# A hybrid decoder block with 32 experts: the gated down biases added to the residual per tile of tokens, in place of a product in each expert

## The chip, the cores and the metric

The kernel runs on one core of one Trainium2 chip. The metric is the device time of one execution in microseconds (us), from the first to the last instruction of the core with what lies around them; smaller is better. Engines are named as the profile names them: PE (TensorE, matrix products), PEld (its weight loads), DVE (VectorE), ACT (ScalarE), POOL (GpSimd) and SP (SyncE, which here only issues transfers). A trailing q (SPq, POOLq, ACTq) is an engine's own instruction queue, DMA issues included. The 16 DMA engines of the core are shared by all queues.

## The reference, cut to what matters

One decoder block on 512 tokens of width 1024 (a gated linear recurrence and a sliding-window attention, merged and projected by `w_out`), and then a mixture of experts: 32 experts, four of which are chosen for each token. All weights are fp32. Of the block's end:

```python
x = x + g1 * (merged @ w_out[l])
h2 = rms_norm(x, norm2_gain[l]) * (1.0 + sc2) + sh2
x = x + g2 * moe_ffn(h2, ...)

def moe_ffn(h, w_router, b_router, w_up, b_up, w_down, b_down):
    logits = (xf @ w_router + b_router).astype(jnp.float32)
    top_vals, top_idx = lax.top_k(logits, TOP_K)          # TOP_K = 4
    gates = jax.nn.softmax(top_vals, axis=-1)
    ...
    def expert_block(args):
        xb, e = args
        hu = xb @ w_up[e] + b_up[e]                        # 1024 -> 2048
        x_glu = jnp.minimum(hu[:, ::2], SWIGLU_LIMIT)
        x_lin = jnp.clip(hu[:, 1::2], -SWIGLU_LIMIT, SWIGLU_LIMIT)
        act = x_glu * jax.nn.sigmoid(SWIGLU_ALPHA * x_glu) * (x_lin + 1.0)
        return act @ w_down[e] + b_down[e]                 # 1024 -> 1024
    ...
    y = jax.ops.segment_sum(y_buf * w_buf[:, None], tok_buf, num_segments=T + 1)[:T]
```

`w_buf` holds the gates. So each expert's bias `b_down[e]` reaches a token's output multiplied by that token's gate for `e` and by `g2`. The sum of these terms over the experts is a product of the gates (512 x 32, four non-zero in a row) with the biases (32 x 1024), and does not depend on the experts' activations.

## The kernel before, in words

**Weights.** Each expert has eight tiles of `w_up` and four of `w_down`, each 1 MB of fp32 as 128 x 2048. SP issues their transfers in the fixed order up 0 to 7 of expert e, then down 0 to 3 of expert e-1, into a ring of slots: nine of `slot`, `NSB` of `slotb` and `NSC` of `slotc`, 18 together. Some of these slots also hold split tiles. A transfer is issued as soon as the slot that it goes into has been released, and SP's queue is in order, so a late release holds back all transfers behind it.

**Splits.** A tile is split into a high fp16 part (ACT, L341 in the helper `split`) and the low rest (DVE, L346), which also releases the fp32 slot. The fourth down tile of an expert is used in fp32 without a split. `ahead(i)` issues the splits up to six places ahead of the tile that PE is about to use.

**An expert on PE.** `up_k` (L1190) is run eight times, with 48 matmuls each; between them stand the selection products of the next expert's tokens (`pick`, L1150). Then `swiglu` runs on DVE and ACT (L1199 to L1216). The down part of expert e-1 comes after the up part of expert e: `down_bias` (L1225), two matmuls that set the two PSUM banks `pd` to the expert's bias, taken from the 64-row table `bd` (high and low fp16 parts of `b_down`, made in `bias_dn`) by a one-hot column of `E64`; then `down_j` (L1241 in fp16, L1233 in fp32) adds to `pd`; `finish` multiplies with gate and `g2row` into `y` (L1253, DVE) and POOL adds up to 96 rows of `y` into the output in memory with an indirect accumulating transfer (L1245).

**The router stage.** It lies between the block's first half and the experts (380 to 445 us). For each of four tiles of 128 tokens, `logits(t)` multiplies by `w_out` (L903, PE), forms the new residual `x1` (L958 to L961, DVE), transposes it (L968, PE; copies L971 on ACT and L972 on DVE), multiplies by the router weights (L976), and writes `x1` to the output (L983, POOL's queue); `choose(t)` and `gates(t)` find the four experts and their gates on DVE (L987 to L1027). The four tiles of `x` are loaded ahead of the loop, each into its own buffer. In this stage `pre(t)` issues a few splits of the first expert's tiles; a scheduler sets the order on each engine.

**Order.** From `mark` on, just behind the router's loop, PE, DVE and ACT run their instructions in the order in which the program writes them. A wait on one of these engines therefore holds everything behind it. POOL and SP are in order too. At the end stands a loop over experts with more than 96 tokens (overflow), which runs no round in these inputs' profile.

Of the kernel before, what the change touches and what calls it, by code (L numbers as in the profile page):

```python
# [10 lines left out]
F32 = mybir.dt.float32  # L11
F16 = mybir.dt.float16
# [29 lines left out]
def block_body(tc, x, c, positions, w_ada, b_ada, norm1_gain, w_in, lower_bound_logits, hg_norm_gain,  # L42
# [19 lines left out]
    with top:  # L62
# [874 lines left out]
        gs = moe.tile([128, NT, 2], F32, name="gs")  # L937
        ge = moe.tile([128, NT, NE], F32, name="ge")
        GS = 1024.0

        x1s, xas, rss = {}, {}, {}

        for t in range(NT):
            x1s[t] = wk.tile([128, D], F32, name=f"x1_{t}")
            A.dma_start(x1s[t], x2[128 * t:128 * t + 128, :])

        def logits(t, pieces):
# [34 lines left out]
            V.scalar_tensor_tensor(lg[:, t, :], bl[:, :NE], rs[:, 2:3], brow, op0=OP.mult, op1=OP.add)  # L982
            G.dma_start(out2[128 * t:128 * t + 128, :], x1)  # L983

# [33 lines left out]
        def gates(t):  # L1018

            V.tensor_sub(gt[:, t], tv[:, t, 0:4], tv[:, t, 0:1].to_broadcast([128, 4]))  # L1020
            A.activation(gt[:, t], gt[:, t], AF.Exp, accum_out=gs[:, t, 0:1])
            V.reciprocal(gs[:, t, 1:2], gs[:, t, 0:1])
            V.tensor_scalar(gt[:, t], gt[:, t], gs[:, t, 1:2], GS, op0=OP.mult, op1=OP.mult)
            V.tensor_mul(oh[:, t], oh[:, t], gt[:, t, :, None].to_broadcast([128, 4, NE]))
            V.tensor_reduce(ge[:, t, :], oh[:, t].rearrange("p k e -> p e k"), axis=AX.X, op=OP.add)
            V.tensor_copy(aux[:, t, :, 1], ge[:, t, :])
            V.tensor_sub(aux[:, t, :, 2], ge[:, t, :], aux[:, t, :, 1])  # L1027

# [3 lines left out]
        SU = SW * SH2  # L1032
        pmod = moe.tile([64, 1], F32, name="pmod")
        G.iota(pmod[0:32], pattern=[[0, 1]], base=0, channel_multiplier=1, allow_small_or_imprecise_dtypes=True)
        G.iota(pmod[32:64], pattern=[[0, 1]], base=0, channel_multiplier=1, allow_small_or_imprecise_dtypes=True)
        E64 = moe.tile([64, NE], F16, name="E64")
        V.tensor_scalar(E64, iota_e[:64, :], pmod[:, 0:1], 32768.0, op0=OP.is_equal, op1=OP.mult)

        SBD = 1.702 * SW * SACT / 32768.0

# [10 lines left out]
        def bias_dn():  # L1051
            st = ready.pop(("bdn",))
            A.activation(bd, st[:64, :1024], AF.Copy, scale=SBD)
            V.scalar_tensor_tensor(bd[32:64], st[32:64, :1024], SBD, bd[32:64], op0=OP.mult, op1=OP.subtract)
            free(st)
# [32 lines left out]
        def select0(t0, t1):  # L1088
            V.tensor_tensor(sel0[:, t0:t1], iota_c[:, None, :C].to_broadcast([128, t1 - t0, C]),
                            pos[:, t0:t1, 0:1].to_broadcast([128, t1 - t0, C]), op=OP.is_equal)  # L1090

        for t in range(NT):
            if t == NT - 1:
                select0(0, NT - 1)
            logits(t, ((0, D),) if t < NT - 1 else LAST)
            pre(t + 1)
            if t < NT - 1:
                choose(t)
                make_h2(t)
                gates(t)  # L1100
        for j in range(4):
            hl_done(("wo", j))
# [119 lines left out]

        def down_bias(one):
            for u in range(2):
                T.matmul(pd[u][:C, :], lhsT=one.to_broadcast([64, C]), rhs=bd[:, 512 * u:512 * u + 512],  # L1225
                         start=True, stop=False)

        def down_j(w, j, act, act32):
            if j == 3:
                for u in range(2):  # L1230
                    for k in (6, 7):
                        o = 1024 * (k % 2) + 512 * u
                        T.matmul(pd[u][:C, :], lhsT=act32[:, k - 4, :], rhs=w[:, o:o + 512],  # L1233
                                 start=False, stop=(k == KT - 1))
                return
            for k in (2 * j, 2 * j + 1):
                o = 1024 * (k % 2)
                for n, (pa_, pw) in enumerate(PASSES):
                    for u in range(2):
                        c0 = 2048 * pw + o + 512 * u  # L1240
                        T.matmul(pd[u][:C, :], lhsT=act[:, pa_, k, :], rhs=w[:, c0:c0 + 512],  # L1241
                                 start=False, stop=False)

# [103 lines left out]
        for e in range(NEX + 1):  # L1347
            if e < NEX:
                prep = nexts.pop(e + 1, iter(()))
                xg = state[e][0]  # L1350
                for k in range(8):
                    ahead(i)
                    if e > 0 and k in PICK_AT:
                        next(prep, None)
                    up_k(hlmap[("up", e, k)], k, xg)
                    hl_done(("up", e, k))
                    if k == 3 and e in TABLE_AT:
                        next(table)
# [20 lines left out]
            if e > 0:  # L1379
                _, gate, idx = state.pop(e - 1)  # L1380
                down_bias(E64[:, e - 1:e])
                for j in range(4):
# [28 lines left out]
        with tc.For_i(0, nreg, 1) as it:  # L1411
# [39 lines left out]
            swiglu(act, act32)  # L1451
            e1h = moe.tile([64, 1], F16, name="ovh")
            V.tensor_scalar(e1h, pmod, col[:64, 0:1], 32768.0, op0=OP.is_equal, op1=OP.mult)
            down_bias(e1h)
            for j in range(4):
# [18 lines left out]
_OUTS = [((1, 512, 1024), 'float32')]  # L1474
NSB, NSC = 5, 4
LOOK = 6
# [29 lines left out]
```

## Time and profile before

| what | value |
|---|---|
| median of 2 runs | 1498.71 us (1497.76 to 1499.66) |
| profiled execution: its own time | 1499.43 us |
| profiled execution: its span | 1497.6 us |
| mean granted clock of TensorE | 0.981 |
| PE / PEld / DVE / ACT / POOL busy, share of the span | 94% / 69% / 87% / 70% / 22% |
| bytes by the hardware queue of the loads (q1) | 458.78 MB, 78.0% of the 16 engines' span |
| mean DMA rate over the span | 318 GB/s |

The execution has three parts: the block's first half (up to about 380 us), the router stage (to about 445 us), and 32 experts (to the end). Shares over the whole span mix them; the views below are therefore cut to stretches. PEclk is the granted clock as a share of 2.4 GHz. A busy PE in the profile is not a PE at its peak, because ends of matmuls are modelled.

### The profile page before, as it was taken

How to read it: one execution, taken by the hardware profiler on the slowest of the kernel's cores; microseconds unless marked ns; L12 is line 12 of the kernel's file. 1: busy time of each engine (PE TensorE's matmuls, PEld its weight loads, DVE VectorE, ACT ScalarE, POOL GpSimd, SP SyncE). 2: the span in 40 equal slices, each digit the busy share in tenths (PEclk: the TensorE clock that was granted, in tenths of full speed). 3: DMA queues.
4: the chain of work that ended last, by engine and by line, in shares of the span. 5: the costliest groups of instructions: out<-in, count | busy, mean ns of one | idle time of the engine just before them, and what ended most of it. 6: DMA issues, size and time to landing. Idle time of an engine off the chain costs nothing. (4 is left out here: it accounts for less than half of the span.)

```text
span 1497.6 us, 41130 instructions
## 1 busy us (share of the span) xinstructions
PE 1405.6 (94%) x18200; PEld 1039.4 (69%) x18200; DVE 1300.0 (87%) x1457; ACT 1054.6 (70%) x1024; POOL 328.4 (22%) x82
## 2 busy tenths in 40 slices
PE   3979999999978999999989999999999999999994
PEld 2536567444558877788777788877788877788871
DVE  6876677777888999999999999999999999999882
ACT  4556334632448888887978888888888888888860
POOL 1020000010110333322322334212044433215300
PEclk9999999999988999999999999999999999999997
DMA  9822321476758999999999999999999999999971
GB/s 315 276 87 85 113 56 57 138 258 231 292 215 308 390 392 411 406 405 398 393 397 367 405 408 411 401 405 400 406 409 401 408 389 403 397 401 409 391 276 16
DMA packets 113520, 476.44 MB, mean 318 GB/s; under 512 B 10717, under 2 KB 35386, under 8 KB 80538
## 3 DMA queue, kind: packets, MB, share of 16 engines
q1 hardware_dynamic: 106160, 458.78, 78.0%
q0 software_dynamic: 5440, 12.72, 3.9%
q8 instruction: 144, 2.36, 0.6%
q10 hardware_dynamic: 1738, 2.27, 0.5%
q14 instruction: 38, 0.31, 0.1%
HBM read 463.22 MB, written 14.70 MB: 319 GB/s over the span
## 5 line engine op out<-in xcount | busy, mean ns | idle before, releaser
L1190 PE MATMUL pu<-xg,slot 128*128 128x96 f16 x10224 | 465.6, 207 | 8.8 <-issue 7.5
L1190 PEld LDWEIGHTS <-slot 128*128 128x128 f16 x10224 | 449.2, 98 | 25.5 <-issue 21.8
L1245 POOL DMA_INDIRECT out_dram<-y,idx x32 | 295.0, 9219 | 754.4 <-DVE y L1253 740.3
L346 DVE SCALAR_TENSOR_TENSOR slot<-slot,slot 128x2048 f16<-128x2048 f32 (+1 forms) x120 | 271.4, 2271 | 30.9 <-ACT slot L341 30.5
L341 ACT ACTIVATE slot<-slot 128x2048 f16<-128x2048 f32 (+1 forms) x120 | 242.0, 2032 | 68.9 <-DVE slot L346 24.1
L346 DVE SCALAR_TENSOR_TENSOR slot<-slotb,slot 128x2048 f16<-128x2048 f32 x101 | 228.0, 2285 | 8.0 <-ACT slot L341 7.7
L346 DVE SCALAR_TENSOR_TENSOR slot<-slotc,slot 128x2048 f16<-128x2048 f32 x97 | 219.6, 2284 | 11.8 <-ACT slot L341 10.5
L341 ACT ACTIVATE slot<-slotc 128x2048 f16<-128x2048 f32 x97 | 201.6, 2105 | 33.7 <-issue 11.5
L341 ACT ACTIVATE slot<-slotb 128x2048 f16<-128x2048 f32 x101 | 197.1, 1956 | 34.5 <-PE pu L1190 14.6
L1241 PEld LDWEIGHTS <-act 128*96 128x96 f16 x1152 | 140.2, 124 | 116.8 <-issue 17.0
L1241 PE MATMUL pd<-slot,act 128*96 128x512 f16 x924 | 206.4, 380 | 0.0
L701 PE MATMUL mm<-hT,slot 128*128 128x512 f16 x672 | 151.4, 380 | 0.0
L701 PEld LDWEIGHTS <-slot 128*128 128x128 f16 x672 | 65.5, 98 | 77.6 <-issue 2.9
L1150 PE MATMUL gb<-sel,h 128*128 128x96 f16 x1984 | 106.9, 208 | 12.8 <-ACT xg L1157 11.1
L1150 PEld LDWEIGHTS <-h 128*128 128x128 f16 x1984 | 93.1, 99 | 12.7 <-issue 12.5
L1190 PE MATMUL pu<-xg,slotb 128*128 128x96 f16 x2064 | 96.0, 207 | 1.8 <-issue 1.8
L1190 PEld LDWEIGHTS <-slotb 128*128 128x128 f16 x2064 | 91.2, 98 | 5.2 <-issue 4.6
L1233 PE MATMUL pd<-slot,act 128*96 128x512 f32 x144 | 64.7, 592 | 0.0
L785 POOL DMA_DIRECT2D mdram<-mr x8 | 4.7, 592 | 269.5 <-DVE mr L779 206.3
L1157 ACT ACTIVATE xg<-gb 128x384 f16<-128x384 f32 x124 | 59.2, 478 | 1.1 <-PE gb L1150 1.1
L1183 ACT ACTIVATE pu<-bu 128x384 f32<-128x384 f32 x128 | 57.2, 480 | 1.0 <-DVE sg_g L1199 1.0
L1253 DVE SCALAR_TENSOR_TENSOR y<-pd,gate,g2row 96x512 f32<-96x512 f32 x64 | 44.9, 739 | 14.0 <-PE pd L1233 14.0
(339 smaller groups left out, 1637.1 us busy)
## 6 DMA issues: line engine op xcount, KB each, us to landing
slotc<-in_w_up_dram SPq DMA_DIRECT2D x116, 1024.0 KB, 15.4
slot<-in_w_up_dram SPq DMA_DIRECT2D x110, 1024.0 KB, 13.9
slotb<-in_w_down_dram SPq DMA_DIRECT2D x98, 1024.0 KB, 17.6
slotb<-in_w_up_dram SPq DMA_DIRECT2D x30, 1024.0 KB, 12.3
slot<-in_w_down_dram SPq DMA_DIRECT2D x20, 1024.0 KB, 22.4
slot<-in_w_in_dram SPq DMA_DIRECT2D x16, 1024.0 KB, 5.3
slot<-in_w_ada_dram SPq DMA_DIRECT2D x16, 1024.0 KB, 5.5
slotc<-in_w_down_dram SPq DMA_DIRECT2D x10, 1024.0 KB
```

The lines of the kernel that those rows point to most:

```text
L341: A.activation(hi, src, AF.Copy, scale=SW)
L346: V.scalar_tensor_tensor(lo, src, SW, hi, op0=OP.mult, op1=OP.subtract)
L701: T.matmul(bk, lhsT=hl[:, o:o + 128], rhs=hT[:, ph, k, :], start=(k == 0 and n == 0), stop=(k == KT - 1 and n == 2))
L785: G.dma_start(mdram[q:q + 1, 512 * u:512 * u + 512], m)
L1150: T.matmul(bk[:, C * k:C * k + C], lhsT=h2[:, part, t, 128 * kk:128 * kk + 128], rhs=sel[:, t, :], start=(k == 0 and t == 0), stop=(t == N ...
L1157: A.activation(xg[:, part, 4 * u:4 * u + 4, :].rearrange("p k c -> p (k c)"), bk[:, :4 * C], AF.Copy)
L1183: A.activation(pu[i][:, :4 * C].rearrange("p (m c) -> p m c", m=4), b[:, 4 * i:4 * i + 4, None].to_broadcast([128, 4, C]), AF.Copy)
L1190: T.matmul(o, lhsT=hl[:, 2048 * pw + 128 * f:2048 * pw + 128 * f + 128], rhs=xg[:, pa_, k, :], start=False, stop=(k == KT - 1 and n == 2), ...
L1233: T.matmul(pd[u][:C, :], lhsT=act32[:, k - 4, :], rhs=w[:, o:o + 512], start=False, stop=(k == KT - 1))
L1241: T.matmul(pd[u][:C, :], lhsT=act[:, pa_, k, :], rhs=w[:, c0:c0 + 512], start=False, stop=False)
L1245: G.indirect_dma_start(out=out2, out_offset=bass.IndirectOffsetOnAxis(ap=idx[:n, :1], axis=0), in_=y[:n, :], in_offset=None, bounds_check= ...
L1253: V.scalar_tensor_tensor(y[:C, sl], pd[u][:C, :], gate[:C], g2row[:C, sl], op0=OP.mult, op1=OP.mult)
```

## The change: gated biases per tile of tokens

The two matmuls of `down_bias` go out of every expert, with `E64` and `pmod`; the first matmul of `down_j` now starts the bank. In their place:

- `bias_dn` first multiplies the bias table by `g2row` (L1075, DVE), so `bd` holds `g2 * b_down`.
- For tiles 0, 1 and 2 of the tokens, `residual(t)` runs behind `gates(t)`: PE transposes the gates (L1033), ACT and DVE make a high and a low part (L1034, L1035), four matmuls of 512 columns multiply them with `bd` (L1041, L1042), DVE adds the two banks to `x1` (L1053), and only then is `x1` written to the output (L1054).
- Tile 3's `x1` is written without the biases, as before. Its bias products are made while expert 1 runs, into the banks `pd`, and added to the output by one more indirect accumulating transfer, of 128 rows.
- `x1` has two buffers for the four tiles. The load of tile t+1 is issued at the start of round t, from ACT's queue; that of tile 2 waits until tile 0 has been written out, that of tile 3 until tile 1 has.
- `slotb` has six slots instead of five and `slotc` three instead of four; the slots of `slotb` exist in the router stage already.
- Expert 0 issues no splits in its last four rounds, and in expert 31 `ahead` stops earlier, so that some splits stand behind the `swiglu` of these experts.

```diff
@@ router stage
-        for t in range(NT):
-            x1s[t] = wk.tile([128, D], F32, name=f"x1_{t}")
+        def load_x1(t):
+            x1s[t] = wk.tile([128, D], F32, name="x1", bufs=2)
             A.dma_start(x1s[t], x2[128 * t:128 * t + 128, :])
...
-            G.dma_start(out2[128 * t:128 * t + 128, :], x1)
+            if t == NT - 1:
+                G.dma_start(out2[128 * t:128 * t + 128, :], x1)
...
+            V.tensor_copy(ge[:, t, 1, :], ge[:, t, 0, :])
+
+        def gates_T(t, bk, gT):
+
+            T.transpose(bk[:64, :128], ge[:, t].rearrange("p u e -> p (u e)"), ident)
+            A.activation(gT[:, 0], bk[:64, :128], AF.Copy)
+            V.tensor_sub(gT[:32, 1], bk[:32, :128], gT[:32, 0])
+
+        def bias_products(gT, bks):
+
+            for u in range(2):
+                sl = slice(512 * u, 512 * u + 512)
+                T.matmul(bks[u], lhsT=gT[:, 0], rhs=bd[:, sl], start=True, stop=False)
+                T.matmul(bks[u], lhsT=gT[:32, 1], rhs=bd[:32, sl], start=False, stop=True)
+
+        def residual(t):
+
+            gT = wk.tile([64, 2, 128], F16, name="gT")
+            gates_T(t, sd_bank(), gT)
+            bks = [sd_bank(), sd_bank()]
+            bias_products(gT, bks)
+            x1 = x1s[t]
+            for u in range(2):
+                sl = slice(512 * u, 512 * u + 512)
+                V.scalar_tensor_tensor(x1[:, sl], bks[u], 1.0 / (GS * SBD), x1[:, sl], op0=OP.mult, op1=OP.add)
+            G.dma_start(out2[128 * t:128 * t + 128, :], x1)
...
         def bias_dn():
             st = ready.pop(("bdn",))
+            V.tensor_mul(st[:64, :1024], st[:64, :1024], g2row[:64])
             A.activation(bd, st[:64, :1024], AF.Copy, scale=SBD)
             V.scalar_tensor_tensor(bd[32:64], st[32:64, :1024], SBD, bd[32:64], op0=OP.mult, op1=OP.subtract)
...
+        load_x1(0)
         for t in range(NT):
             if t == NT - 1:
                 select0(0, NT - 1)
+            if t < NT - 1:
+                load_x1(t + 1)
             logits(t, ((0, D),) if t < NT - 1 else LAST)
             pre(t + 1)
             if t < NT - 1:
                 choose(t)
                 make_h2(t)
                 gates(t)
+                residual(t)
@@ experts
-        def down_bias(one):
-            for u in range(2):
-                T.matmul(pd[u][:C, :], lhsT=one.to_broadcast([64, C]), rhs=bd[:, 512 * u:512 * u + 512],
-                         start=True, stop=False)
...
                         T.matmul(pd[u][:C, :], lhsT=act[:, pa_, k, :], rhs=w[:, c0:c0 + 512],
-                                 start=False, stop=False)
+                                 start=(k == 0 and n == 0), stop=False)
...
                 for k in range(8):
-                    ahead(i)
+                    if e == NEX - 1:
+                        ahead(min(i, len(order) - 5 - LOOK))
+                    elif e > 0 or k < 4:
+                        ahead(i)
...
+                    if e == 1 and k == 1:
+                        gT = moe.tile([128, 4 * C], F32, name="sg_l").bitcast(F16)[:64, :256]
+                        gT = gT.rearrange("p (q n) -> p q n", q=2)
+                        gates_T(NT - 1, pd[0], gT)
+                    if e == 1 and k == 3:
+                        bias_products(gT, pd)
+                        y = moe.tile([128, D], F32, name="y")
+                        for u in range(2):
+                            V.tensor_scalar(y[:, 512 * u:512 * u + 512], pd[u], 1.0 / (GS * SBD), None, op0=OP.mult)
+                        rix = moe.tile([128, 1], I32, name="idx", bufs=4)
+                        G.iota(rix, pattern=[[0, 1]], base=128 * (NT - 1), channel_multiplier=1)
+                        add_out(y, rix, 128)
...
-                down_bias(E64[:, e - 1:e])
...
-NSB, NSC = 5, 4
+NSB, NSC = 6, 3
```

The first place is DVE in the router stage, behind the gates of tile 0 (`ge`, `aux`); `rs` are the small steps of tile 1's norm, `xat` the low part of its transposed tile. Of the kernel before:

```order
L1025 TENSOR_REDUCE ge<-oh 128x32
L259 TENSOR_SCALAR rs<-rs 128x1
L1026 CAST aux<-ge 128x32
L260 TENSOR_SCALAR rs<-rs 128x1
L1027 TENSOR_TENSOR aux<-ge,aux 128x32
L972 TENSOR_TENSOR xat<-sd,xat 128x512
L261 TENSOR_SCALAR rs<-rs 128x1
L262 TENSOR_SCALAR rs<-rs 128x1
L265 TENSOR_SCALAR rs<-rs 128x1
```

And of the change:

```order
L1027 CAST aux<-ge 128x32
L1029 COPY ge<-ge 128x32
L260 TENSOR_SCALAR rs<-rs 128x1
L1028 TENSOR_TENSOR aux<-ge,aux 128x32
L261 TENSOR_SCALAR rs<-rs 128x1
L262 TENSOR_SCALAR rs<-rs 128x1
L265 TENSOR_SCALAR rs<-rs 128x1
L269 SCALAR_TENSOR_TENSOR rs<-rs 128x1
L1035 TENSOR_TENSOR gT<-sd,gT 32x128
...
L1053 SCALAR_TENSOR_TENSOR x_2893<-sd,x_2893 128x512 x2
L972 TENSOR_TENSOR xat<-sd,xat 128x512
```

A copy of the gates (L1029), the low part of the transposed gates (L1035, which needs PE and ACT first) and two additions to tile 0's `x1` (L1053, which need the bias products) now stand among tile 1's steps, and the copy of `xat` behind them.

The second place is ACT's queue in the router stage, in the change, with the waits: `x_3044` and `x_3194` are the `x1` of tiles 2 and 3, `DMASW2` and `DMASW3` the landing of POOL's writes of tiles 0 and 1.

```order
L1005 ACTIVATE h_2220<-xa 128x1024 [waits DVE_49]
L945 DMA x_3044<-in_x_dram 128x1024 [waits DMAHW0_49,DMASW2_49]
L1022 ACTIVATE gt,gs<-gt 128x4 [waits DVE_49]
L1034 ACTIVATE gT<-sd 64x128 [waits PE_49,Activation_49]
L963 ACTIVATE sqt,rs<-x_3044 128x1024 [waits DMAHW0_49,DVE_49]
L971 ACTIVATE xat<-sd 128x512 [waits PE_49,Activation_49] x2
L945 DMA x_3194<-in_x_dram 128x1024 [waits DMAHW3_49,DMASW3_49,DVE_49]
```

The loads of tiles 2 and 3 stand ahead of the exponential of a later tile's gates (L1022), and the copies of `gT` and `xat` behind it; before, all four loads stood ahead of the first tile's work.

The third place is DVE at the end of expert 31: L1199 and L1226 open its `swiglu`, L1253 and L1275 are the results of experts 30 and 31. Of the kernel before:

```order
L346 SCALAR_TENSOR_TENSOR slotb_2806<-slot_63,slotb_2806 128x2048
L346 SCALAR_TENSOR_TENSOR slotb_2807<-slot_70,slotb_2807 128x2048
L1199 TENSOR_SCALAR sg_g<-pu_3465 128x384
L1199 TENSOR_SCALAR sg_g<-pu_3466 128x384
...
L1216 SCALAR_TENSOR_TENSOR act<-act_21740,act 128x192
L346 SCALAR_TENSOR_TENSOR slot_71<-slotc_3544,slot_71 128x2048
L1253 SCALAR_TENSOR_TENSOR y<-pd_3469,gate,g2row 96x512
L1253 SCALAR_TENSOR_TENSOR y<-pd_3470,gate,g2row 96x512
```

And of the change:

```order
L346 SCALAR_TENSOR_TENSOR slotc_3586<-slotb_2809,slotc_3586 128x2048
L1226 TENSOR_SCALAR sg_g<-pu_3505 128x384
L1226 TENSOR_SCALAR sg_g<-pu_3506 128x384
...
L1243 SCALAR_TENSOR_TENSOR act<-act_21731,act 128x192
L346 SCALAR_TENSOR_TENSOR slot_68<-slot_69,slot_68 128x2048
L346 SCALAR_TENSOR_TENSOR slotb_2807<-slot_64,slotb_2807 128x2048
L346 SCALAR_TENSOR_TENSOR slot_67<-slot_63,slot_67 128x2048
L1275 SCALAR_TENSOR_TENSOR y<-pd_3509,gate,g2row 96x512
```

The splits of the first two down tiles of expert 31 have moved from ahead of its `swiglu` to behind it. Expert 0's `swiglu` moves the other way round the splits too: between the selection matrix for expert 1 (L1172, now L1199) and this `swiglu` stand nine splits in the kernel before and four in the change.

## Rows read from the trace of the kernel before

**Rows 1.** Windows; columns: stretch, length, busy time per engine, granted clock, DMA share, rate.

```profile
400.00:410.00 10.00, 8.00 (x44) 3.98 (x43) 9.96 (x21) 5.08 (x7) 3.84 (x2) 1.00 0.04 16
492.00:554.00 62.00, 62.00 (x996) 50.06 (x994) 60.26 (x51) 53.84 (x47) 22.55 (x2) 1.00 1.00 398
833.00:864.00 31.00, 31.00 (x500) 25.03 (x498) 30.07 (x26) 26.97 (x24) 12.03 (x1) 1.00 1.02 405
1468.00:1475.00 7.00, 6.54 (x15) 2.82 (x15) 0.98 (x2) 0.00 (x0) 1.43 (x1) 0.50 0.23 33
```

**Rows 2.** DMA view, 1000 to 1130 us: queue, packets, MB, share; issues with us to landing.

```profile
q1 hardware_dynamic: 9079, 51.21, 96.5%
q0 software_dynamic: 448, 1.14, 4.4%
...
slotb<-in_w_down_dram SPq DMA_DIRECT2D x13, 1024.0 KB, 20.2
```

**Rows 3.** DMA view, 480 to 483 us: one load on idle queues, with us to landing.

```profile
slotc<-in_w_up_dram SPq DMA_DIRECT2D x1, 1024.0 KB, 4.8
```

**Rows 4.** Timeline of PE, one down part: start, length, line, operation, count.

```profile
787.36 0.63 PE L1225 MATMUL pd<-bd,E 64*96 64x512 f16 x2
787.92 5.38 PE L1241 MATMUL pd<-slot,act 128*96 128x512 f16 x24
```

**Rows 5.** Timeline of DVE, router stage; in brackets: idle before and its releaser.

```profile
387.91 1.29 DVE L958 SCALAR_TENSOR_TENSOR xa<-mm,rrow 128x512 f32<-128x512 f32 x2 [5.00 <-PE mm L903]
...
394.85 0.69 DVE L972 TENSOR_TENSOR xat<-sd,xat 128x512 f16<-128x512 f32 x1 [0.38 <-ACT xat L971]
...
399.76 1.28 DVE L1003 SCALAR_TENSOR_TENSOR xa<-xa,rs,rrow 128x1024 f32<-128x1024 f32 x1
...
410.51 0.20 DVE L1026 CAST aux<-ge 128x32 f16<-128x32 f32 x1
...
417.80 0.68 DVE L960 TENSOR_TENSOR x<-x,xa 128x512 f32<-128x512 f32 x1
...
424.23 0.69 DVE L958 SCALAR_TENSOR_TENSOR xa<-mm,rrow 128x512 f32<-128x512 f32 x1 [1.61 <-PE mm L903]
```

**Rows 6.** DMA view, 374 to 440 us, issues: KB each, median us to landing.

```profile
x<-in_x_dram ACTq DMA_DIRECT2D x4, 512.0 KB, 6.8
...
g2row<-mdram POOLq DMA_DIRECT2D x1, 512.0 KB, 9.6
```

**Rows 7.** DMA view, 404 to 415 us: a write of `x1` on idle queues.

```profile
out_dram<-x POOLq DMA_DIRECT2D x1, 512.0 KB, 3.4
```

**Rows 8.** DMA view, 386 to 396 us: the same write beside weight loads.

```profile
out_dram<-x POOLq DMA_DIRECT2D x1, 512.0 KB, 9.6
```

**Rows 9.** Timeline of POOL: issue of the load of `g2row`.

```profile
380.19 0.55 POOL L885 DMA_DIRECT2D g2row<-mdram  x1 [4.29 <-DMA mdram<-mr]
```

**Rows 10.** Timeline of DVE around the `swiglu` of expert 0.

```profile
472.28 1.01 DVE L1199 TENSOR_SCALAR sg_g<-pu 128x384 f32<-128x384 f32 x2
...
478.90 4.50 DVE L346 SCALAR_TENSOR_TENSOR slot<-slotc,slot 128x2048 f16<-128x2048 f32 x2 [0.96 <-ACT slot L341]
```

**Rows 11.** Timeline of DVE at the end.

```profile
1458.06 2.29 DVE L346 SCALAR_TENSOR_TENSOR slotb<-slot,slotb 128x2048 f16<-128x2048 f32 x1 [1.03 <-ACT slotb L341]
1460.27 1.02 DVE L1199 TENSOR_SCALAR sg_g<-pu 128x384 f32<-128x384 f32 x2
...
1465.38 2.29 DVE L346 SCALAR_TENSOR_TENSOR slot<-slotc,slot 128x2048 f16<-128x2048 f32 x1 [1.28 <-ACTq L1411]
1467.59 1.40 DVE L1253 SCALAR_TENSOR_TENSOR y<-pd,gate,g2row 96x512 f32<-96x512 f32 x2
```

**Rows 12.** Timeline of PE at the end.

```profile
1458.64 3.60 PE L1233 MATMUL pd<-slot,act 128*96 128x512 f32 x8
1468.38 1.24 PE L1225 MATMUL pd<-bd,E 64*96 64x512 f16 x2 [6.14 <-DVE y L1253]
1469.55 8.14 PE L1241 MATMUL pd<-slotb,act 128*96 128x512 f16 x24
```

More of the change, by code (lines that the diff above doesn't have):

```diff
@@ L937, in block_body @@
         gs = moe.tile([128, NT, 2], F32, name="gs")
-        ge = moe.tile([128, NT, NE], F32, name="ge")
+        ge = moe.tile([128, NT, 2, NE], F32, name="ge")
         GS = 1024.0
         x1s, xas, rss = {}, {}, {}
-        for t in range(NT):
-            x1s[t] = wk.tile([128, D], F32, name=f"x1_{t}")
+        def load_x1(t):
+            x1s[t] = wk.tile([128, D], F32, name="x1", bufs=2)
             A.dma_start(x1s[t], x2[128 * t:128 * t + 128, :])
@@ L1024, in gates @@
             V.tensor_mul(oh[:, t], oh[:, t], gt[:, t, :, None].to_broadcast([128, 4, NE]))
-            V.tensor_reduce(ge[:, t, :], oh[:, t].rearrange("p k e -> p e k"), axis=AX.X, op=OP.add)
-            V.tensor_copy(aux[:, t, :, 1], ge[:, t, :])
-            V.tensor_sub(aux[:, t, :, 2], ge[:, t, :], aux[:, t, :, 1])
+            V.tensor_reduce(ge[:, t, 0, :], oh[:, t].rearrange("p k e -> p e k"), axis=AX.X, op=OP.add)
+            V.tensor_copy(aux[:, t, :, 1], ge[:, t, 0, :])
+            V.tensor_sub(aux[:, t, :, 2], ge[:, t, 0, :], aux[:, t, :, 1])
+            V.tensor_copy(ge[:, t, 1, :], ge[:, t, 0, :])
[18 more added lines that the diff above has]
+            G.dma_start(out2[128 * t:128 * t + 128, :], x1)
         bu = moe.tile([128, NE, 16], F32, name="bu")
@@ L1032, in block_body @@
         SU = SW * SH2
[L1033 to L1039, printed above, removed]
+        SBD = 16.0
         def bias_up():
@@ L1451, in block_body @@
             swiglu(act, act32)
-            e1h = moe.tile([64, 1], F16, name="ovh")
-            V.tensor_scalar(e1h, pmod, col[:64, 0:1], 32768.0, op0=OP.is_equal, op1=OP.mult)
-            down_bias(e1h)
             for j in range(4):
```

## Prediction

> **What bounds the kernel now.** I first cut the execution into windows and read busy times beside the DMA share. The reader is to see that no single engine answers for the whole. From 400 to 410 us DVE is busy 9.96 of 10 us and the 16 DMA engines 0.04; in the expert part they change places with a share of 1.00 to 1.02, while PE is busy for 62.00 of 62 and for 31.00 of 31 us as well [rows 1]. So in the expert part two resources look full, and the change takes work from one of them. Next came the DMA view of a stretch in the middle: the weight loads move 51.21 MB in 130 us, and a load lands 20.2 us after its issue [rows 2], against 4.8 us on idle queues [rows 3]. So several earlier loads always wait in the queues: (20.2 - 4.8) us at 2.66 us a load (below) are about six. An expert has twelve loads of 1.049 MB, 12.58 MB; at 51.21/130 = 0.394 MB per us they take 31.9 us, 2.66 each. PE needs 31.00 us for 500 matmuls and an expert has 498, so 30.9 us; DVE is busy 30.07 of the same 31 [rows 1]. DMA is the slowest, by 1.0 us per expert; PE can run full only by eating up the lead of loaded slots. The end is set by when the DMA engines start to run without gaps, the number of bytes from there, and what follows the last load. The router stage, where DVE is full and DMA stands, sets the first; the timelines of DVE and PE at the end show the third.
>
> **The change, part by part.** The sum is made against the profiled execution's 1499.43 us, 0.7 us above the median of 1498.71 of the runs shown.
>
> *Bias products out of the experts.* L1225 starts at 787.36 and the next line at 787.92: 0.56 us [rows 4]. In 32 experts that is 17.9 us less on PE, and PE's need falls from 30.9 to 30.3 us. I cost this at nothing, since the loads' 31.9 us cover it; without that cover it would be the whole 17.9 us.
>
> *Bias table times `g2row`.* `g2row` is issued at 380.19 [rows 9] and lands 9.6 us later [rows 6], at 389.8. Before, DVE's next work began at 387.91, behind 5.00 us of idle time, in which the making of `bd` lay hidden [rows 5]. Now L1075 must wait for `g2row` on DVE, with tile 0's first additions behind it: 1.9 us, or nothing if `g2row` lands sooner because two of the four `x` loads no longer run beside it. I take the middle, 1.0. L1075 and L1077 cover 1024 columns as the 1.28 us row does [rows 5], 1.2 us each by their pitch. Sum 3.4 us, ends 2.4 and 4.3.
>
> *Per tile, three times, on DVE.* Two additions of 512 columns, as the pair at 387.91, 1.29 us; a copy of 32 columns and the low part of the gates, 0.20 us each by the row of the 32-column copy [rows 5]: 1.7 us, 5.1 in all. Then two waits per tile for PE and ACT (transpose and copy; products). The nearest row is the 0.38 us for an ACT copy [rows 5]: six of these are 2.3 us, but small steps of the next tile stand in between, so 1.5; ends 0 and 3. PE and ACT have idle time there and cost nothing more. Of the existing gaps DVE can fill part, such as 1.61 us at 424.23 [rows 5]: minus 1.0, ends 0 and minus 3.1, which grants as much again for gaps that have no row here. Sum 5.6 us.
>
> *Two buffers for `x1`.* The load of tile 2 waits for tile 0's write, and ACT, in order, waits with it: the exponential of tile 1's gates stands behind. The chain is the issue 0.55 [rows 9], a write of 3.4 us on idle queues [rows 7], and a load for which I take the same 3.4: 7.4 us. From the gates of tile 0 at 410.51 to the first addition of tile 2 at 417.80 DVE worked 7.3 us [rows 5]; with the half of tile 1's work that now comes behind L1053 I count about 8. So nothing, with 1 us as upper end; the case of busy queues is a rival. The Trainium skill, page "DMA: Bandwidth & Descriptors", section "Anatomy of one DMA", prices a transfer at 2.0 us plus its bytes at 436 KB per us, which for 512 KB makes 3.2 us. By it no tile would stall; the trace agrees on idle queues with 3.4 us, and not beside weight loads.
>
> *One slot more in the router stage.* One load earlier is worth 1.049/0.394 = 2.7 us if the DMA engines never run dry after it. They do: at about 481 us a load meets empty queues [rows 3]. So nothing; lower end minus 2.7.
>
> *Splits around the `swiglu` of expert 0.* It opened at 472.28, and splits went on at 478.90, 6.6 us later [rows 10]. With five splits of 2.2 us moved behind, it could open at 461.3, and the five end at 461.3 + 6.6 + 11.0 = 478.9: no change, unless PE has not yet finished the last up tile and DVE idles. I take plus 1.0, ends 0 and 2.5.
>
> *The added accumulating transfer.* Four of them take 4.4% of 130 us and 1.14 MB [rows 2], 1.43 us and 0.285 MB each. The new one has 128 rows of 4 KB, 0.52 MB: 2.6 us of full DMA engines, ends 1.4 and 2.8.
>
> *The end.* Before, `swiglu` of expert 31 waited until 1460.27 behind a split that waited for its load; a third split followed at 1465.38, and `y` of expert 30 came at 1467.59, for which PE waited 6.14 us [rows 11, 12]. With `swiglu` ahead of the splits, the third can follow the second at once: it began 7.3 us after it [rows 11] and needs only 2.2, less what ACT's high parts take behind `swiglu`, about 1.2. That makes 3.9 us; PE's expert 30 ends at 1462.2 [rows 12] and forbids more than 5.3. L1225 with its 1.24 us at this place goes too: minus 5.1 in all. If PE's shorter pause leaves its clock at 2.4 GHz, the 24 matmuls that took 8.14 us at a granted 0.50 [rows 1, 12] take 5.38 [rows 4]: up to 2.8 us more. I don't count that. Ends minus 3 and minus 8.
>
> Sum: 3.4 + 5.6 + 0 + 1.0 + 2.6 - 5.1 = +7.5 us; 1499.4 + 7.5 = **1507 us**, 0.55% above the median. With all ends on one side: 2.4 + 2.0 + 0 - 2.7 + 1.4 - 8 = -4.9, so 1494.5; and 4.3 + 8.1 + 1 + 2.5 + 2.8 - 3 = +15.7, so 1515.
>
> **The rivals.** *PE sets the pace.* If loads could run faster whenever PE asks for them faster, all 17.9 us come back: 1507 - 17.9 = 1489 us. For it speaks PE's busy time; against it the 20.2 us from issue to landing, since queues with six loads in them already run as fast as they can. By the Trainium skill, page "Perfetto Trace Analysis", section "Identifying the Most-Contended Engine", the occupancy of 16 DMA engines misleads and the rate is to be read; page "DMA: Bandwidth & Descriptors", section "Measured", has 425 GB/s for a large transfer, so the 405 here would leave 5%. The landing times of this trace speak against that room. Chance 0.09.
>
> *The router stage hides it.* If the scheduler puts the new steps wholly into DVE's gaps and `g2row` lands early, the router costs 2 us in place of 9.0: 1500 us. Against it: DVE's 9.96 of 10 us. Chance 0.17.
>
> *The write of `x1` stalls its next load (slower).* Beside weight loads a write takes 9.6 [rows 8] and a load 6.8 us [rows 6]: 0.55 + 9.6 + 6.8 = 17 us against 8 of cover, 9 us for tile 2 and again for tile 3: 1507 + 18 = 1525 us. It decides as soon as write and load together exceed about 7.5 us. For it: the tenth early load lengthens the traffic into this stage, and ACT is held too. Against it: the DMA share of 0.04 from 400 us on. Chance 0.12.
>
> That the products stay in the experts is excluded by the program: no line multiplies `bd` in the experts but tile 3's.
>
> **How the numbers follow.** Forecast 0.62, rivals 0.09, 0.17 and 0.12. The likeliest case has 1494 to 1515 us. The range reaches to 1490 on the side of the PE rival and to 1520 on that of the stalled loads, and leaves out about half of the first, most of the second and the ends of the likeliest, 0.2 together. A difference of 2% (30 us) is about what a measurement of this kernel tells from no change. Faster by that needs 1469 us, which no case reaches: 0.02. Slower by it needs 1529, which only the stalled loads with further delay reach: 0.04. Within 2%: 0.94.
>
> **What would show it.** Right: the first gapless loads come some 10 us later than before, twelve loads still take 31.9 us, PE shows gaps in the experts, and PE's pause before the last down part shrinks to some 2 us. Wrong: loads per expert faster than 31.9 us; idle time of DVE ahead of L960 for tiles 2 and 3; a router stage as long as before; or DMA engines that run dry for longer after expert 0's `swiglu`.

## The result and the profile after

The changed kernel takes 1522.31 us (median of 2 runs, 1521.99 to 1522.63) against 1498.71: ratio 1.0149, interval 1.0133 to 1.0165 (the two medians alone give 1.0157). The forecast was 1507, its range ended at 1520: slower than forecast by 15 us, and 2 us outside the range.

To see where the time went, I cut each profiled execution at four marks that every version has: the issue of the first of the 384 weight loads of the experts (SP), DVE's step that makes the router's values `lg` of tile 3, the issue of the 38th weight load (in expert 2 to 3, when the loads run without gaps), and that of the 382nd (the third down tile of expert 31). Each entry is a difference of two starts in one trace, in us.

| kernel | to first load | first load to `lg(3)` | `lg(3)` to 38th load | 38th to 382nd load | 382nd load to end | span |
|---|---|---|---|---|---|---|
| before | 364.6 | 75.5 | 71.2 | 922.3 | 64.0 | 1497.6 |
| after | 365.5 | 95.4 | 78.5 | 923.4 | 57.9 | 1520.7 |
| after less before | +0.9 | +19.9 | +7.3 | +1.0 | -6.0 | +23.1 |

The first column, which the change does not touch, tells how far two executions differ anyhow: 364.3 to 366.9 over all versions. The last but two points to what paces the experts: 344 loads take 922.3 us before and 923.4 after, 2.68 us each, though PE is busy for 15 us less in that stretch (890.32 us in place of 905.50). So the loss sits in the router stage and in experts 0 and 1, and a gain at the end.

**The router stage.** Timeline of DVE of the changed kernel, start, length, line, operation, in brackets the idle time before and what ended it. `L1075` is the bias table times `g2row`, `L960` the addition to `x1`; the row at 428.97 is tile 2, that at 449.45 tile 3.

```profile
385.34 1.22 DVE L1075 TENSOR_TENSOR slot<-slot,g2row 64x1024 f32<-64x1024 f32 x1
390.50 0.69 DVE L958 SCALAR_TENSOR_TENSOR xa<-mm,rrow 128x512 f32<-128x512 f32 x1 [3.94 <-PE mm L903]
...
428.97 0.68 DVE L960 TENSOR_TENSOR x<-x,xa 128x512 f32<-128x512 f32 x1
...
438.76 0.25 DVE L982 SCALAR_TENSOR_TENSOR lg<-sd,rs,brow 128x32 f32<-128x32 f32 x1
...
449.45 0.69 DVE L960 TENSOR_TENSOR x<-x,xa 128x512 f32<-128x512 f32 x1 [8.99 <-DMA x<-in_x_dram]
...
460.92 0.25 DVE L982 SCALAR_TENSOR_TENSOR lg<-sd,rs,brow 128x32 f32<-128x32 f32 x1
```

`g2row` makes nobody wait here: `L1075` starts without idle time (in x1_four it waits 0.43 us), and what DVE waits for next is PE, as before the change [rows 5]. Tile 2's addition has no bracket. Tile 3's has 8.99 us, and the releaser is its own load. The queues show why; here POOL, ACT and SP of the changed kernel:

```profile
433.26 0.58 POOL L1054 DMA_DIRECT2D out_dram<-x  x1 [8.74 <-DVE x L1053]
```

```profile
434.37 0.60 ACT L971 ACTIVATE xat<-sd 128x512 f16<-128x512 f32 x1 [1.13 <-PE sd L968]
441.52 0.33 ACTq L945 DMA_DIRECT2D x<-in_x_dram  x1
441.96 2.01 ACT L341 ACTIVATE slot<-slotb 128x2048 f16<-128x2048 f32 x1 [6.99 <-DMA out_dram<-x]
```

```profile
433.34 2.70 SPq L158 DMA_DIRECT2D slot<-in_w_up_dram  x3
436.64 27.68 SPq L158 DMA_DIRECT2D slotc<-in_w_up_dram  x3
```

Tile 1's `x1` is written from 433.26 on. ACT stands behind this write until 441.52, and only then issues tile 3's load, which lands 7.9 us later. Both transfers, 8.2 and 7.9 us, are more than twice as long as a write on idle queues (3.4 us, [rows 7]), and SP starts weight loads again at 433.34: PE has done with the first `w_out` tiles (SP's wait of 44.7 us ended with `L903`), and their slots come free. The windows (columns as in [rows 1]) show the same as a change of traffic in the middle of the stage:

```profile
410.00:430.00 20.00, 15.66 (x99) 7.63 (x97) 17.37 (x51) 4.62 (x11) 4.04 (x3) 0.91 0.15 53
430.00:440.00 10.00, 6.60 (x71) 4.53 (x70) 9.21 (x30) 2.50 (x5) 0.58 (x1) 0.95 0.53 184
440.00:450.00 10.00, 0.18 (x1) 0.00 (x0) 0.98 (x3) 3.15 (x4) 2.11 (x1) 0.50 1.01 426
490.00:552.00 62.00, 53.30 (x911) 45.72 (x912) 57.21 (x41) 51.74 (x41) 14.33 (x2) 0.89 0.85 318
862.00:893.00 31.00, 30.92 (x509) 25.34 (x506) 30.46 (x26) 27.45 (x24) 14.57 (x2) 1.00 1.02 408
```

From 440 to 450 us DVE is busy 0.98 of 10 us and PE 0.18, and TensorE's granted clock is 0.50, its lower level of 1.2 GHz. The DMA share is 1.01: not the queues, but the work stands.

**Experts 0 and 1.** After the change `lg(3)` comes 20.8 us later (460.92 in place of 440.12), so the same work is to be compared 20.8 us later too. Of the kernel before, 62 us from 29 us behind `lg(3)` on:

```profile
469.00:531.00 62.00, 60.55 (x1008) 52.26 (x1008) 58.61 (x56) 52.82 (x51) 12.15 (x1) 0.92 0.93 356
```

Against the row of 490 to 552 us above, the DMA share falls from 0.93 to 0.85: by estimate 0.08 x 62 = 5 us more in which the loads could have run. In the DMA view, 40 slices of 1.5 us each show the holes, first of the kernel before from 469 to 529 us, then of the changed kernel from 490 to 550:

```profile
DMA  9999992047999899999999968999999999999999
```

```profile
DMA  9700496685036999999999999999899999999999
```

DVE of the changed kernel opens expert 0's `swiglu` at 481.39, and then waits:

```profile
481.39 1.02 DVE L1226 TENSOR_SCALAR sg_g<-pu 128x384 f32<-128x384 f32 x2 [1.89 <-PE pu L1217]
...
486.67 0.15 DVE L1192 TENSOR_SCALAR idx<-gb 96x1 int32<-96x1 f32 x1 [3.26 <-ACT xg L1184]
...
491.28 2.29 DVE L346 SCALAR_TENSOR_TENSOR slot<-slotb,slot 128x2048 f16<-128x2048 f32 x1 [0.94 <-ACT slot L341]
```

```profile
483.53 0.49 ACT L1184 ACTIVATE xg<-gb 128x384 f16<-128x384 f32 x1 [5.86 <-PE gb L1177]
```

```profile
491.31 0.26 PE L1217 MATMUL pu<-xg,slot 128*128 128x96 f16 x1 [5.57 <-ACT slot L341]
```

Three engines wait one for another: DVE for ACT's copies of expert 1's selected tokens (`xg`), ACT for PE's selection products, and PE then for the splits, which begin again at 491.28, 9.9 us after `swiglu` opened (6.6 before, [rows 10]). The loads show what that costs: counted from `lg(3)`, the 23rd is issued after 21.9 us and the 24th only after 34.9 (before: 27.9 and 30.1).

**The end.** DVE and PE of the changed kernel:

```profile
1480.90 1.01 DVE L1226 TENSOR_SCALAR sg_g<-pu 128x384 f32<-128x384 f32 x2
...
1486.01 2.29 DVE L346 SCALAR_TENSOR_TENSOR slot<-slot,slot 128x2048 f16<-128x2048 f32 x1 [1.28 <-ACT slot L341]
1488.21 2.28 DVE L346 SCALAR_TENSOR_TENSOR slotb<-slot,slotb 128x2048 f16<-128x2048 f32 x1
1490.42 2.28 DVE L346 SCALAR_TENSOR_TENSOR slot<-slot,slot 128x2048 f16<-128x2048 f32 x1
1492.62 1.40 DVE L1275 SCALAR_TENSOR_TENSOR y<-pd,gate,g2row 96x512 f32<-96x512 f32 x2
```

```profile
1493.51 4.56 PE L1263 MATMUL pd<-slot,act 128*96 128x512 f16 x12 [5.69 <-DVE y L1275]
```

Against [rows 11] the splits follow `swiglu` without a wait for a load, and the time from the 382nd load to the end falls from 64.0 to 57.9 us.

### The profile page after: what moved, and what is told of

The parts are those of the page before. It is cut to its first block, busy times and chain, and to the rows that moved or that the text cites. A ratio compares the mean times of both kernels' runs of the same rounds, so it can differ in the third digit from the quotient of the medians.

```text
span 1520.7 us, 41073 instructions
## 1 busy us (share of the span) xinstructions
PE 1393.5 (92%) x18156; PEld 1034.6 (68%) x18156; DVE 1304.7 (86%) x1473; ACT 1052.9 (69%) x1028; POOL 397.7 (26%) x82
## 3 DMA queue, kind: packets, MB, share of 16 engines
q1 hardware_dynamic: 106160, 458.78, 76.7%
## 5 line engine op out<-in xcount | busy, mean ns | idle before, releaser
L1267 POOL DMA_INDIRECT out_dram<-y,idx x33 | 365.5, 11077 | 683.0 <-DVE y L1275 615.8
L346 DVE SCALAR_TENSOR_TENSOR slot<-slot,slot 128x2048 f16<-128x2048 f32 (+1 forms) x122 | 276.3, 2271 | 37.7 <-ACT slot L341 37.2
L341 ACT ACTIVATE slot<-slot 128x2048 f16<-128x2048 f32 (+1 forms) x122 | 246.5, 2032 | 86.8 <-DVE slot L346 26.2
L346 DVE SCALAR_TENSOR_TENSOR slot<-slotb,slot 128x2048 f16<-128x2048 f32 x123 | 277.3, 2284 | 12.8 <-ACT slot L341 11.0
L341 ACT ACTIVATE slot<-slotb 128x2048 f16<-128x2048 f32 x123 | 242.7, 1979 | 58.5 <-DMA slotb<-in_w_up_dram 12.8
L1263 PE MATMUL pd<-slot,act 128*96 128x512 f16 x936 | 210.1, 382 | 5.7 <-DVE y L1275 5.7
L346 DVE SCALAR_TENSOR_TENSOR slot<-slotc,slot 128x2048 f16<-128x2048 f32 x73 | 165.0, 2282 | 5.2 <-ACT slot L341 5.2
L341 ACT ACTIVATE slot<-slotc 128x2048 f16<-128x2048 f32 x73 | 151.8, 2110 | 13.0 <-PE pu L1217 4.2
L1217 PE MATMUL pu<-xg,slotb 128*128 128x96 f16 x2112 | 100.0, 208 | 4.7 <-ACT pu L1210 2.2
L1184 ACT ACTIVATE xg<-gb 128x384 f16<-128x384 f32 x124 | 59.2, 478 | 6.7 <-PE gb L1177 6.7
L346 DVE SCALAR_TENSOR_TENSOR slotb<-slotb,slotb 128x2048 f16<-128x2048 f32 x24 | 54.8, 2283 | 3.5 <-ACT slotb L341 3.5
```

What stands on the lines that cost most here:

```text
L341: A.activation(hi, src, AF.Copy, scale=SW)
L346: V.scalar_tensor_tensor(lo, src, SW, hi, op0=OP.mult, op1=OP.subtract)
L1184: A.activation(xg[:, part, 4 * u:4 * u + 4, :].rearrange("p k c -> p (k c)"), bk[:, :4 * C], AF.Copy)
L1217: T.matmul(o, lhsT=hl[:, 2048 * pw + 128 * f:2048 * pw + 128 * f + 128], rhs=xg[:, pa_, k, :], start=False, stop=(k == KT - 1 and n == 2), ...
L1267: G.indirect_dma_start(out=out2, out_offset=bass.IndirectOffsetOnAxis(ap=idx[:n, :1], axis=0), in_=y[:n, :], in_offset=None, bounds_check= ...
```

## The experiments

Each is timed beside the kernel before, on the same chip; the ratio compares these two, and can differ from that of the medians by 0.001. Three chips were used; the kernel before has medians of 1499.23, 1499.53 and 1500.18 us on them, so medians of two versions can be compared across chips to about 1 us. The marks of all versions first, in us as in the table above:

| kernel | first load to `lg(3)` | `lg(3)` to 38th load | 38th to 382nd | 382nd to end | median | ratio to before |
|---|---|---|---|---|---|---|
| x1_four | 84.3 | 79.1 | 923.3 | 57.9 | 1513.01 | 1.0088 (1.0065 to 1.0111) |
| x1_sp | 87.3 | 81.0 | 922.1 | 59.9 | 1517.71 | 1.0120 (1.0105 to 1.0135) |
| exp0_ahead | 95.8 | 71.9 | 924.6 | 59.2 | 1519.25 | 1.0132 (1.0113 to 1.0151) |
| tile3_late | 96.8 | 76.7 | 926.5 | 58.7 | 1524.64 | 1.0163 (1.0145 to 1.0182) |
| four_exp0 | 84.3 | 72.3 | 924.2 | 57.6 | 1506.88 | 1.0040 (1.0029 to 1.0051) |
| four_exp0_nores | 76.5 | 72.0 | 924.5 | 57.6 | 1498.50 | 0.9989 (0.9979 to 0.9999) |
| four_exp0_not3 | 84.2 | 70.8 | 923.7 | 58.6 | 1505.00 | 1.0032 (1.0020 to 1.0043) |
| four_exp0_notail | 85.4 | 73.5 | 923.6 | 61.5 | 1509.25 | 1.0055 (1.0038 to 1.0072) |
| before_nobias | 75.4 | 71.2 | 923.5 | 61.0 | 1499.22 | 0.9999 (0.9988 to 1.0009) |
| before_tail | 75.3 | 70.3 | 923.3 | 58.8 | 1494.95 | 0.9970 (0.9956 to 0.9983) |

**x1_four: a buffer of its own for each tile of `x1`.** The change with `bufs=4`; `NSB, NSC` go back to 5, 4, since the added buffers take their room, and so the extra early slot goes too.

```diff
-            x1s[t] = wk.tile([128, D], F32, name="x1", bufs=2)
+            x1s[t] = wk.tile([128, D], F32, name="x1", bufs=4)
...
-NSB, NSC = 6, 3
+NSB, NSC = 5, 4
```

> The changed kernel with four buffers for x1 in place of two; to make room, slotb and slotc go back to five and four slots. Theory (the load of tile 3's x1 waits for tile 1's write, and both then share the DMA engines with weight loads): the 8.99 us of idle time of DVE ahead of tile 3's first addition is gone, and the time falls from 1522.3 to about 1513 us. Rival 1 (DVE would have waited for PE or ACT at this place anyway, or its work only shifts): 1519 to 1522. Rival 2 (the slot given back was worth a load): 9 us come back and 2.7 are lost, 1516.

It gives back 9.3 us. The router stage shrinks by 95.4 - 84.3 = 11.1 us: the 8.99 us of waiting for tile 3's load, and 2.1 us less of DVE's waits for `L903` (3.5 us in place of 5.6). The traffic is the same, and DVE now works through it; its windows from 440 to 450 us:

```profile
440.00:450.00 10.00, 5.80 (x34) 2.88 (x33) 7.76 (x28) 1.64 (x4) 1.71 (x3) 0.50 0.99 402
```

So the weight loads did no harm by themselves, only through a load that had to be made among them. Two edits are in this run, and the slots were not tested alone. What they could move is when loads are issued, and behind the router the 38th load comes 79.1 us after `lg(3)` with the old slots and 78.5 with the new ones: 0.6 us, not 9.

**x1_sp: tile 3's load on SP's queue.** The change, with the wait for tile 1's write taken off ACT's queue. On SP the load stands behind two of the five weight loads of this stretch and ahead of three, not behind three and ahead of two as I had expected.

```diff
-            A.dma_start(x1s[t], x2[128 * t:128 * t + 128, :])
+            (A if t < 3 else nc.sync).dma_start(x1s[t], x2[128 * t:128 * t + 128, :])
```

> The changed kernel with the load of tile 3's x1 issued from SP's queue in place of ACT's; there it stands behind three of the weight loads of this stretch and ahead of two, which wait with it. Theory (the write of tile 1 and this load are long because weight loads run beside them): the write still lands at about 441.5 us, the load behind it then runs nearly alone, 3.4 us in place of 7.9, so DVE's 8.99 us of idle time become about 4.5 and the time 1518 us. Rival (the time goes because ACT is held): with ACT free and the load issued at the same time, the idle time stays near 9 us only if the load does; a time of 1513 would say that ACT's hold was all of it, 1522 that traffic beside the load is not the cause.

The total came out as expected, by another way. DVE waits 0.89 us for the load in place of 8.99:

```profile
444.20 0.69 DVE L960 TENSOR_TENSOR x<-x,xa 128x512 f32<-128x512 f32 x1 [0.89 <-DMA x<-in_x_dram]
```

With the weight loads held behind `x1`'s load, and ACT free, the router stage is 8.1 us shorter than after the change, still 3.0 longer than with four buffers; the stretch to the 38th load is 2.5 us longer, which I put down to the held loads. Two things changed at once. The load lands 4.1 us after its issue (440.13 to 444.20) in place of 7.9, and some 4 us of steps for tile 2's gates (439.06 to 443.32), which after the change came behind tile 3's addition, now stand ahead of it. So the order among the transfers makes the stall; how much of it the crowded load made, and how much the held ACT, this run does not part.

**exp0_ahead: expert 0 issues its splits in all rounds.** The change without its exception for expert 0.

```diff
-                    elif e > 0 or k < 4:
+                    else:
```

> The changed kernel with splits issued in all eight rounds of expert 0 again. Theory (between the swiglu of expert 0 and that of expert 1 DVE idles 3.3 us behind ACT's copies, 1.9 us for PE, and more behind the high parts, because no split stands ready there): the stretch between the two swiglus, 44.1 us after the change and 25.2 before, comes back near 27, and the time falls by about 5 us to 1517. Rival (as predicted: the splits only change places, at most 1 to 2.5 us): 1520 to 1522.

The stretch from `lg(3)` to the 38th load falls from 78.5 to 71.9 us, 6.6, as between x1_four and four_exp0 (79.1 to 72.3, 6.8). The median falls by 3.1 only, and the intervals overlap; in its profile the stall is 9.32 us, and the stretch behind the 382nd load, the tail, 1.3 us longer. This run alone doesn't show the gain in the time, the next one does. With the splits ahead, `swiglu` of expert 0 opens 12.6 us later than after the change, at 493.98, and that of expert 1 5.5 us earlier, at 520.03. The loads follow the second: the 24th is issued 29.9 us after `lg(3)` in place of 34.9, and the 38th 5.5 us earlier (533.88 in place of 539.41).

**four_exp0: both at once.** Four buffers, and splits ahead in expert 0.

> The changed kernel with both repairs: four buffers for x1 (slots 5 and 4) and splits in all rounds of expert 0. Theory (the two losses lie behind one another and add up): 1513.0 - 3 to 6 = 1507 to 1510 us. Rival (they cover each other): 1513.

The losses add up: -9.3 by the buffers, then -6.1 by the order (x1_four 1513.01, four_exp0 1506.88). In the DMA view from 480 to 540 us, again 29 us behind `lg(3)`, the holes are back to about those of the kernel before:

```profile
DMA  9979996007999997989999999999999999999999
```

What is left, 7.4 us over the kernel before on that chip (1499.53) by the medians and 4.3 to 7.6 by the interval, is the change with neither of its two ordering losses (and without its extra early slot), close to the 7.5 of the forecast.

**four_exp0_nores: no bias work on tiles 0 to 2.** four_exp0 without `gates_T`, the products and additions for these tiles.

> The kernel with both repairs and without the transposed gates, products and additions of tiles 0 to 2 (their down biases are left out of the output); the writes stay where they are. Theory (the router stage is bound by DVE, and each tile's 1.7 us and its waits lie on the path): 5.1 to 6.6 us less than the kernel with both repairs. Rival (the scheduler puts them into gaps): less than 1.5 us.

8.4 us less, 7.8 of it in the router stage (84.3 to 76.5). I had 5.6. DVE's busy time in the stage differs by 5.1 us (71.55 and 66.44), as priced; its idle time differs by 2.7 (12.75 and 10.05), where I had 1.5 - 1.0 = 0.5. The largest part of that is 1.7 us behind ACT's copies of `xat` in place of 0.2. The rest of the stage, 76.5 against 75.5 before, leaves 1.0 us for the bias table and the copy of the gates, which stays; for the table I had 3.4.

**tile3_late and four_exp0_not3: the products of tile 3.** The first moves them from expert 1 to expert 12, the second leaves them and the transfer out.

```diff
-                    if e == 1 and k == 1:
+                    if e == 12 and k == 1:
...
-                    if e == 1 and k == 3:
+                    if e == 12 and k == 3:
```

> The changed kernel with tile 3's bias products and their 128-row transfer in expert 12 in place of expert 1. Theory (in expert 1 they hold PE for 5.1 us behind a step of DVE that stands behind splits, at a place where the DMA engines still run dry; in expert 12 the loads cover it): 3 us less, 1519. Rival (only the transfer's bytes cost, and they are the same at both places): 1522.

> four_exp0 without the product of tile 3 in expert 1, its scaling by the gates and the 128-row transfer that adds it (so the down biases of tile 3's tokens are left out). Theory: the transfer moves bytes through a stage that the weight loads fill, so the loads come 2.4 to 2.6 us earlier from expert 1 on and the end with them: 1506.9 - 2.5 = 1504.4. Rival: the transfer finds room beside the loads and costs nothing: 1507.

The move gained nothing: the stretch ahead of the 38th load is 1.8 us shorter, the one behind it, where the products now stand, 3.1 longer, and the median is 2.3 higher. So of the 3 us that I expected from PE's wait in expert 1 nothing shows. Leaving the products and the transfer out moves the two stretches by -1.6 and -0.5 us, near the 2.6 us forecast for 128 rows. The intervals around 1.0032 and 1.0040 overlap and don't decide it, and the stretch from the 38th to the 382nd load varies by 2.5 us among the other versions (922.1 to 924.6). So a cost of some 2 us fits, but is not shown. That the cost is the bytes, and not the number of rows, was not tested.

**four_exp0_notail and before_tail: the limit at the end alone.** Taken out of four_exp0, and put alone into the kernel before.

```diff
-                    ahead(i)
+                    ahead(min(i, len(order) - 5 - LOOK) if e == NEX - 1 else i)
```

> four_exp0 with the limit of the splits ahead in the last expert as it was before the change (all else as four_exp0). Theory: the new limit gives 5 to 6 us at the end, behind the last landing, whatever came earlier: 1506.9 + 5 = 1512, with the last landing where four_exp0 has it and the tail after it about 41 us. Rival: with later loads the old limit does no harm: 1507.

> The kernel before with one part of the change alone: in expert 31 ahead stops earlier, so that the splits of its first two down tiles stand behind its swiglu. Theory (from the last load's landing to the end the change takes 35.3 us in place of 41.6, by this order and by the absence of the bias matmuls, 1.2 us of it): 4 to 5 us less than before, 1494.5. Rival (only PE's clock or the absent matmuls shortened the end): 1498.

Without the limit the tail grows from 57.6 to 61.5 us, and PE's pause ahead of the last down part from 5.70 to 8.59:

```profile
1483.03 7.48 PE L1263 MATMUL pd<-slotb,act 128*96 128x512 f16 x24 [8.59 <-DVE y L1275]
```

The medians say 2.4 us, with overlapping intervals, and the traces 3.9, less than the 5 expected. In the kernel before it gives 4.6 (1499.53 to 1494.95), clear of noise, and that kernel is the fastest of all.

**before_nobias: the kernel before without the products in the experts.** `L1225` goes, and the down biases with it; nothing is put in their place, and the first matmul of `down_j` starts the bank.

> The kernel before with the two bias matmuls of L1225 left out of every expert and nothing in their place (the experts' down biases are left out of the output). Theory (the loads set the pace): no change within 1.5 us, 1497 to 1499; PE shows the 17.9 us as gaps, and a load lands as long after its issue as before. Rival (PE sets the pace): 1498.7 - 17.9 = 1481.

Nothing in the time: 0.9999. 17.9 us of PE, taken from an engine that was busy for 31.00 of 31 us, are worth less than 1.8 us, by the lower end of the interval, 0.9988. PE shows them as gaps: over the same 344 loads it is busy for 890.79 of 923.47 us, before for 905.50 of 922.34.

## Why the prediction was wrong, step by step

**Failed: "Two buffers for `x1` ... So nothing, with 1 us as upper end".** It measured 9.3 us by x1_four and 11.1 in the traces. For tile 2 the term was right: its load was issued 3.34 us after tile 0's write (417.98 to 421.32), and DVE did not wait. For tile 3 the rival's price was right: 0.55 + 9.6 + 6.8 = 17 us, and the addition came 16.2 us after tile 1's write was issued; DVE had work for 7.2 us of them (433.26 to 440.46; I had a cover of 8), which leaves the 8.99 of the trace. Wrong was where I looked for the traffic. Against the rival I set the DMA share of 0.04 "from 400 us on", a window that ends at 410 us [rows 1]. The transfers of tile 3 fall into 433 to 450 us, and the kernel before showed traffic there:

```profile
430.00:440.00 10.00, 4.82 (x55) 3.33 (x53) 9.29 (x37) 4.36 (x10) 2.68 (x2) 0.71 0.98 378
```

The price of a transfer that the prediction cites (the Trainium skill, page "DMA: Bandwidth & Descriptors", section "Anatomy of one DMA") is stated there for POOL's path, which the write takes and the load does not. By an estimate from it the write needs 3.2 us; beside weight loads it took 8.2.

I had put the danger in the tenth early load, at the start of the stage; it was PE's release of the `w_out` slots, at its end. So the rival was priced at 18 us with a chance of 0.12, and half of it came true. That its 1525 us lie 3 us from the measured time is luck: it counted tile 2 as well, and knew nothing of the next loss.

**Failed: "Splits around the `swiglu` of expert 0 ... plus 1.0, ends 0 and 2.5".** It is 6 to 7 us in the traces and 6.1 by four_exp0. The opening was right: 461.3 and the 20.8 us by which the first split behind the router came later (444.67 to 465.48) make 482.1; it opened at 481.39. I then carried over the 6.6 us from there to the next split. But those 6.6 us belonged to a `swiglu` before which PE had nearly made the selection products; opened 11 us earlier, it found ACT waiting for them. The exception that I had named, DVE idle because PE is not through, is what happened: 1.89 us for the last up tile, then 3.26 behind ACT's copies. And the end of the five splits was the wrong mark. It came 2.7 us later than the sum had it (the fifth ran from 500.19 to 502.48, against 478.9 + 20.8 = 499.7), but each of the five releases a slot, and the first of these slots came free 12 us later (32.7 us behind `lg(3)` against 20.7 with the splits ahead). At the 24th load the loss was 5.0 us (34.9 against 29.9).

**Mis-sized: the router's terms.** 9.0 us in all, 8.8 measured (84.3 - 75.5). But 1.0 in place of 3.4 for the table, since DVE waits for PE there in any case (5.00 us before, 4.15 in four_exp0), and 7.8 in place of 5.6 per three tiles: the gaps that I let DVE fill for -1.0 were not filled, idle time grew. The sum was right by luck, because the two errors cancel.

**Right: PE's saving at nothing.** before_nobias settles it: the rival of PE setting the pace is refuted, with 1499.22 us against 1481. In every version the 344 loads from the 38th to the 382nd take 922 to 927 us, with PE's work in them differing by 1.7%. The growth of a load's time (15.9 to 20.2 us in the view of [rows 2], by kind of tile, of which I took the largest, against 4.8 in [rows 3]) had said so, and PE's busy share had not. That DVE, busy for 879 of those 922 us, does not set the pace was not tested by a run; the DMA share of 1.01 over them speaks for the loads.

**Not refuted: the added transfer, 2.6 us.** Two traces give 3.1 and 2.1, about what two executions differ by. **Right in size: the end, -5.1.** The table has -6.0. Counted from the 382nd load, `y` of expert 30 comes 4.1 us earlier (29.8 in place of 33.9), where I had 3.9; `L1225` is gone with 1.2; and the 24 matmuls behind take 1.0 less, at a mean granted clock of 0.75 in place of 0.65, the part that I did not count. One of its signs failed: PE's pause did not shrink to 2 us but is 5.69, since PE comes to expert 30's end 3.6 us earlier too, as it does in before_nobias (28.6 us after the 382nd load before, 25.0 in both).

**The signs.** Of those named for a right forecast, twelve loads still take 32.2 us and PE shows gaps, but the gapless loads came 28 us later in place of some 10. Of those named for a wrong one, two came: idle time ahead of `L960` (for tile 3, not for tile 2), and DMA engines that run dry for longer. The forecast of 1507 stands for the change without its two ordering losses (four_exp0, 1506.88), with the luck of the router's terms in it. That 9.3 and 6.1 us on top give the measured time again is no further proof, since both were taken from the same three medians.

## What to carry to other kernels

Price a buffer's reuse at the time at which its transfers will run, tile by tile, and ask which engine's finish sets other transfers free at that moment; a quiet window 30 us earlier says nothing about it. Where loads set the pace, judge a reordering by when it frees the slots, not by when the step on show opens. An engine that is busy all the time is not the bound until work taken from it shortens the run; the growth of a load's time from issue to landing told it here without a run.

## What the runs showed of the hardware that was not expected

A small step on DVE can take more than ten times its time beside POOL's product of 1024 columns, and ends with it. Of the changed kernel, DVE and POOL at the same moment:

```profile
422.42 2.13 DVE L990 CAST tf<-ti 128x4 f32<-128x4 uint32 x1
```

```profile
422.40 2.12 POOL L1006 TENSOR_TENSOR h<-xa,h 128x1024 f16<-128x1024 f32 x1 [3.83 <-ACT h L1005]
```

The same cast took 0.17 us at 439.56. With four buffers it is a step of 0.69 us (`L960`) that took 2.52 beside POOL's second product at 423.33, and the kernel before has one as well (a step of 4 columns, 2.04 us). In every version each of these products that met a busy DVE stretched one of its steps. Added up, three such steps take 5.6 us more than the same steps elsewhere in four_exp0 and 5.0 in four_exp0_nores, so they make 0.6 us at most of the 2.2 us by which the per-tile term was too small. By the same count they cost 4.6 us before the change and 3.7 after it, in a stage that DVE nearly fills. What the two engines share was not tested.

A transfer that waits in an engine's queue holds the engine's computing: ACT stood idle for 6.99 us ahead of its split at 441.96, behind the load of tile 3. With that load on SP's queue (x1_sp) the same split waited 1.68 us, for PE:

```profile
435.31 2.05 ACT L341 ACTIVATE slot<-slotb 128x2048 f16<-128x2048 f32 x1 [1.68 <-PE mm L903]
```
